# A four-layer diffusion trunk on one core: the gated MLP's preparation in four steps, two early weights for the last feed forward, and three more modulations of layer 2 on TensorE

## The chip, the cores and the metric

The kernel runs on one core of one Trainium2 chip. The metric is the device time of one launch in microseconds (us). Five engines run their own instruction streams and wait for one another: TensorE (PE, with its weight loads as PEld), VectorE (DVE), ScalarE (ACT), GpSimd (POOL) and SyncE (SP), which here issues the DMA transfers. Each engine takes its instructions strictly in program order, so what stands behind a waiting instruction waits too.

## The reference

A trunk of four layers over a sequence of 256 tokens and a context of 256 tokens, 1024 channels, all in float32. Each layer has a mixer (pooling, attention, a state-space model, a gated MLP in turn) and a feed forward with a convolution. Both are framed by modulations that a condition vector makes.

```python
for layer in range(DEPTH):                       # pool, attn, ssm, gmlp
    sh1, sc1, gt1, sh2, sc2, gt2 = split(silu(c) @ ada_w[layer] + ada_b[layer], 6)
    h = x * (1 + sc1) + sh1
    y = mixer[layer](h)
    x = layer_norm(ALPHA * x + gt1 * y)
    f = conv_ffn(x * (1 + sc2) + sh2)
    x = layer_norm(ALPHA * x + gt2 * f)
    # the context stream goes the same way while a later layer reads it

def conv_ffn(h):                                 # 1024 -> 2 * 2816 -> 1024
    a = conv3(h @ w_up) + conv_b
    return (a[:2816] * silu(a[2816:])) @ w_down

def gmlp_mixer(h):                               # chunks of 128 tokens, 8 heads
    u, v = split(gelu(h @ w_in + b_in), 2)
    v = layer_norm(v)
    gate = einsum('hpq,bnqhc->bnphc', w_s, v) + b_s
    return (u * gate) @ w_out
```

`silu(c) @ ada_w` is six products of a 1024-vector with a 1024x1024 matrix per layer; (l, m) below is product m of layer l.

## The kernel before, in words

Every large product is computed as three: a weight is split into a rounded high part wH (ACT, L170) and the rest wL (DVE, or POOL where the call says so, L171), the left side likewise into hH and hL (L527, L528), and `mm3` runs hH·wH, hL·wH and hH·wL (L229, L230, L231). `weight()` issues each weight's load on SP (L186) into one of four `raw` buffers and splits it into one of three slots; pieces are 128x1024 numbers, 512 KB. A list `self.early` can hold weights that were split before their turn. `ahead()` makes such weights out of other tiles: three `araw` buffers and one `gate` buffer, with the low part split on POOL.

The stages follow one another as layer 0's pooling and feed forward, attention, feed forward 1 (ffn(1), 750 to 1187 us), the state-space mixer (to 1326), feed forward 2 (to 1530), the gated MLP (to 1728) and feed forward 3 (to the end).

Two background queues run beside the feed forwards. `hook()` is called once per weight and takes steps from them by credits. The first queue holds the modulations (`ada_task`): each step loads 128 rows of `ada_w` into an `araw` buffer (L327; three buffers, which `ahead` also uses). Where `array(l, m)` is true, TensorE multiplies the rows by the condition two steps later (L320, `ada<-araw,cond`, four matmuls per step). Where it is false, VectorE multiplies and sums them (`adaS`: L337 for the first, L339 for the other seven), and one last step on TensorE adds over the partitions (L320, `adaS,ones`). The second queue (`ssm_tasks`) prepares the state-space mixer: chains of complex products on POOL (`ef`, `efp`, L1176 to L1183) that begin with a load of `prm`, and whose results TensorE reads (L1387, L1388, L1406). All of it has to be done when ffn(1) ends. The last products of ffn(1) lie in 1170 to 1187 us.

`gmlp_open` prepares what the gated MLP needs of `w_s`: the matrix wsn is transposed in two halves on TensorE (L1672), copied by ACT (L1674), split into wsH and wsL, and summed by a product with ones (L1678, copied by L1679). It is called whole before pair 2 of ffn(2).

`out_proj_steps` runs a mixer's last projection and the layer norm behind it (transposes L506, hH and hL), after which the next feed forward begins with `first_up`.

## Time and profile before

| what | value |
|---|---|
| median of 3 runs | 1935.31 us (1934.91 to 1938.88) |
| profiled execution's own time | 1940.46 us |
| its span, first to last instruction | 1938.7 us |
| mean granted TensorE clock | 0.96 |
| busy: PE | 1782.9 us (92%) |
| busy: PEld | 1466.6 us (76%) |
| busy: DVE | 1318.2 us (68%) |
| busy: ACT | 781.3 us (40%) |
| busy: POOL | 1080.3 us (56%) |

Busy time is an average over the stages. A stage is decided by the engine whose chain ends last there, which need not be the one that is busiest over the whole span. The granted clock is the share of full speed that the chip gave TensorE. A row of the timeline has start, duration, engine, line and tiles, and in brackets the idle time ahead of it with the instruction that ended that idle time.

### The profile page before, as it was taken

How to read it: one execution, taken by the hardware profiler on the slowest of the kernel's cores; microseconds unless marked ns; L12 is line 12 of the kernel's file. 1: busy time of each engine (PE TensorE's matmuls, PEld its weight loads, DVE VectorE, ACT ScalarE, POOL GpSimd, SP SyncE). 2: the span in 40 equal slices, each digit the busy share in tenths (PEclk: the TensorE clock that was granted, in tenths of full speed). 3: DMA queues.
4: the chain of work that ended last, by engine and by line, in shares of the span. 5: the costliest groups of instructions: out<-in, count | busy, mean ns of one | idle time of the engine just before them, and what ended most of it. 6: DMA issues, size and time to landing. Idle time of an engine off the chain costs nothing.

```text
span 1938.7 us, 31709 instructions
## 1 busy us (share of the span) xinstructions
PE 1782.9 (92%) x12188; PEld 1466.6 (76%) x12188; DVE 1318.2 (68%) x1853; ACT 781.3 (40%) x1289; POOL 1080.3 (56%) x1040
## 2 busy tenths in 40 slices
PE   6899999899999999999989998688899988979997
PEld 4687676677789878777767776458798878979997
DVE  4565545546677767654676747987879798778666
ACT  2253223224346644422422332234654454436553
POOL 2278104989862335751189998647654444246643
PEclk8899999999999999999989999889899989989999
DMA  9555565565321124566656556865878765547662
GB/s 365 185 156 183 174 190 181 197 206 184 121 87 38 45 80 100 180 189 187 210 194 220 177 186 207 250 222 182 267 273 276 254 222 186 171 154 262 205 188 85
DMA packets 241785, 360.28 MB, mean 186 GB/s; under 512 B 43353, under 2 KB 164825, under 8 KB 241634
## 3 DMA queue, kind: packets, MB, share of 16 engines
q1 hardware_dynamic: 241634, 358.26, 57.2%
q8 instruction: 96, 1.57, 0.3%
q14 instruction: 55, 0.45, 0.1%
HBM read 330.92 MB, written 27.29 MB: 185 GB/s over the span
## 4 chain that ended last, share of the span: by engine, by line
PE 56%; POOL 21%; DVE 11%; issue 4%; DMA 4%; ACT 2%; SPq 0%; POOLq 0%; DVEq 0%; ACTq 0%
PE ps L229 15%; PE ps L230 14%; PE ps L231 14%; POOL ef L1178 2%; DVE wL L171 2%; POOL efp L1182 2%; POOL ef L1181 2%; POOL ef L1183 2%; POOL cv L1824 2%; POOL ef L1176 2%; POOL efp L1177 2%; PE sc L991 1%; PE ps L939 1%; PE ada L320 1%; PE pv L1046 1%
## 5 line engine op out<-in xcount | busy, mean ns | idle before, releaser
L171 DVE TENSOR_TENSOR wL<-raw,wH 128x1024 fp32r<-128x1024 f32 x292 | 422.8, 1453 | 197.2 <-ACT wH L170 189.9
L229 PE MATMUL ps<-hH,wH 128*128 128x256 f32 (+1 forms) x1568 | 524.2, 335 | 9.9 <-ACT wH L170 5.5
L170 ACT ACTIVATE wH<-raw 128x1024 fp32r<-128x1024 f32 x341 | 358.2, 1056 | 419.2 <-PE ps L231 218.3
L231 PE MATMUL ps<-hH,wL 128*128 128x256 f32 (+1 forms) x1568 | 516.8, 330 | 4.5 <-DVE wL L171 4.5
L230 PE MATMUL ps<-hL,wH 128*128 128x256 f32 (+1 forms) x1568 | 518.0, 331 | 1.6 <-DVE hL L528 1.1
L229 PEld LDWEIGHTS ps<-hH,wH 128*128 128x128 f32 x1568 | 301.7, 193 | 52.1 <-issue 8.9
L231 PEld LDWEIGHTS ps<-hH,wL 128*128 128x128 f32 x1568 | 301.5, 193 | 31.3 <-DVE wL L171 4.8
L230 PEld LDWEIGHTS ps<-hL,wH 128*128 128x128 f32 x1568 | 302.6, 193 | 26.7 <-POOL xa L633 1.3
L1824 POOL TENSOR_TENSOR cv<-cv,cv 128x512 f32<-128x512 f32 (+1 forms) x88 | 110.2, 1257 | 224.8 <-ACT cv L1823 224.8
L229 PE MATMUL ps<-wH,gH 128*128 128x512 f32 (+1 forms) x552 | 220.6, 400 | 9.0 <-DVE cv L1796 7.2
L231 PE MATMUL ps<-wH,gL 128*128 128x512 f32 (+1 forms) x552 | 213.9, 392 | 2.4 <-POOL gL L1828 2.3
L230 PE MATMUL ps<-wL,gH 128*128 128x512 f32 (+1 forms) x552 | 215.8, 391 | 0.0
L171 POOL TENSOR_TENSOR wL<-raw,wH 128x1024 fp32r<-128x1024 f32 x49 | 127.2, 2596 | 110.1 <-ACT wH L170 90.0
L1793 ACT ACTIVATE cv<-ps,cw 128x512 f32<-128x512 f32 (+1 forms) x176 | 115.9, 666 | 164.1 <-PE ps L231 138.9
L1794 DVE SCALAR_TENSOR_TENSOR cv<-ps,cw,cv 128x510 f32<-128x510 f32 (+1 forms) x176 | 106.5, 609 | 106.1 <-ACT cv L1793 105.9
L339 DVE SCALAR_TENSOR_TENSOR adaS<-araw,cond,adaS 128x1024 f32<-128x1024 f32 x70 | 117.0, 1671 | 36.2 <-DMA araw<-in_ada_w_dram 36.0
L229 PEld LDWEIGHTS ps<-wH,gH 128*128 128x128 f32 x552 | 106.0, 192 | 41.1 <-issue 15.8
L231 PEld LDWEIGHTS ps<-wH,gL 128*128 128x128 f32 x552 | 105.8, 192 | 26.8 <-POOL gL L1828 3.3
L230 PEld LDWEIGHTS ps<-wL,gH 128*128 128x128 f32 x552 | 106.1, 192 | 21.0 <-issue 0.2
L1796 DVE SCALAR_TENSOR_TENSOR cv<-ps,cw,cv 128x510 f32<-128x510 f32 (+1 forms) x176 | 106.7, 612 | 4.3
L540 POOL TENSOR_SCALAR rs<-mv 128x1 f32<-128x1 f32 x26 | 8.2, 314 | 165.5 <-DVE mv L538 165.0
L1827 ACT ACTIVATE gH<-cv 128x512 fp32r<-128x512 f32 (+1 forms) x88 | 45.9, 521 | 117.6 <-POOL cv L1824 117.6
(434 smaller groups left out, 3322.9 us busy)
## 6 DMA issues: line engine op xcount, KB each, us to landing
araw<-in_ada_w_dram SPq DMA_DIRECT2D x184, 512.0 KB
raw<-in_ffn_w_up_dram SPq DMA_DIRECT2D x176, 512.0 KB
raw<-in_ffn_w_down_dram SPq DMA_DIRECT2D x88, 512.0 KB
raw<-in_gmlp_w_in_dram SPq DMA_DIRECT2D x32, 512.0 KB
fD<-ef SPq DMA_DIRECT2D x16, 512.0 KB
eD<-eo SPq DMA_DIRECT2D x16, 512.0 KB
raw<-in_gmlp_w_out_dram SPq DMA_DIRECT2D x16, 512.0 KB
raw<-in_attn_w_qkv_dram SPq DMA_DIRECT2D x12, 512.0 KB
```

Source lines behind the costliest of these rows:

```text
L170: self.nc.scalar.activation(h, x, AF.Copy)
L171: (eng or self.nc.vector).tensor_tensor(l, x, h.bitcast(F32), op=ALU.subtract)
L229: mm(ps, lhsT=w[0], rhs=x[0], start=first, stop=False)
L230: mm(ps, lhsT=w[0], rhs=x[1], start=False, stop=False)
L231: mm(ps, lhsT=w[1], rhs=x[0], start=False, stop=last)
L339: nc.vector.scalar_tensor_tensor(a, raws[k], self.cond[:, k, r:r + 1], a, op0=ALU.mult, op1=ALU.add)
L1176: eng.tensor_tensor(out[0], a[0], b[0], op=ALU.mult)
L1793: nc.scalar.activation(c, p3, AF.Identity, scale=cw[:, 1, h:h + 1], bias=cw[:, 3, h:h + 1])
L1794: nc.vector.scalar_tensor_tensor(c[:, :, 1:], p3[:, :, :255], cw[:, 0, h:h + 1], c[:, :, 1:], op0=ALU.mult, op1=ALU.add)
L1796: nc.vector.scalar_tensor_tensor(c[:, :, :255], p3[:, :, 1:], cw[:, 2, h:h + 1], c[:, :, :255], op0=ALU.mult, op1=ALU.add)
L1824: nc.gpsimd.tensor_tensor(cv[0, j], cv[0, j], cv[1, j], op=ALU.mult)
L1827: nc.scalar.activation(gH, c0, AF.Copy)
```

## The change

It has three parts, called (a), (b) and (c) below.

(a) `array` becomes true for (2, 2), (2, 3) and (2, 4). These three modulations, which VectorE summed in ffn(1), are made by TensorE.

(b) The gated MLP's preparation becomes a generator in four steps, taken before pairs 1, 2, 3 and 4 of ffn(2). The matrix wsn lies in a `gate` buffer and not in a `raw` buffer, and is loaded at the start; the copies lie in an `h32` tile.

(c) `out_proj_steps` also calls `ahead` for the gated MLP's last projection (where there are no extra slots), so the first two weights of ffn(3) are loaded and split into three `araw` buffers and one `gate` buffer while that projection runs.

```diff
     def array(self, l, m):
-        return l < 2 or l == 2 and m < 2
+        return l < 2 or l == 2 and m < 5
...
             if hf:
                 self.conv(l)
-            if hf and S == 2:
+            if hf and (S == 2 or not self.extra):
                 ahead = self.ahead([w for w, shape in self.first_up(l, 2)])
...
+        if S == 2 or not self.extra:
+            self.early = ahead
         if S == 2:
-            self.early = ahead
             self.post_T(made["n"][0])
...
         def steps():
+            wsn = self.t(self.main, [128, D], F32, "gate", 3).rearrange("p (h q) -> p h q", h=8)
+            nc.sync.dma_start(wsn, I["gmlp_w_s"][0].rearrange("h p q -> p h q"))
...
-            wsn = self.t(self.wp, [128, 8, 128], F32, "raw", 4)
-            nc.sync.dma_start(wsn, I["gmlp_w_s"][0].rearrange("h p q -> p h q"))
...
+            yield
             for i in range(2):
...
-                w32 = self.t(self.sm, [128, 512], F32, "tmp", 3)
+                w32 = self.t(self.sm, [128, 4, 128], F32, "h32", 2).rearrange("p a b -> p (a b)")
                 nc.scalar.activation(w32, ps, AF.Copy)
+                yield
...
-        self.between = steps
+        self.between = steps()
...
-                    if p == 2 and self.between:
-                        self.between()
-                        self.between = None
+                    if p and self.between:
+                        next(self.between, None)
```

In the changed file the lines behind L299 have numbers higher by one to four: L1672 is L1675 there, L1678 is L1682, L1794 is L1797, L1828 is L1831.

**Part (a): DVE and PE in ffn(1).** DVE in the program before, in the last products of ffn(1)'s up projection, where (2, 2) ends and (2, 3) begins:

```order
L1828 TENSOR_TENSOR gL_9126<-cv_1532_9011,gH_9125 128x512
L1796 SCALAR_TENSOR_TENSOR cv_1551_9119<-ps_9020,cw_7122,cv_1551_9119 128x2x255
L171 TENSOR_TENSOR wL_9293<-raw_9290,wH_9292 128x1024
L339 SCALAR_TENSOR_TENSOR adaS_9079<-araw_9483,cond_94,adaS_9079 128x1024
L1828 TENSOR_TENSOR gL_9132<-cv_1533_9015,gH_9131 128x512
L1794 SCALAR_TENSOR_TENSOR cv_1573_9232<-ps_9135,cw_7122,cv_1573_9232 128x2x255
L337 TENSOR_SCALAR adaS_9576<-araw_9577,cond_94 128x1024
L1796 SCALAR_TENSOR_TENSOR cv_1573_9232<-ps_9135,cw_7122,cv_1573_9232 128x2x255
```

The same place on DVE in the changed program:

```order
L1831 TENSOR_TENSOR gL_9125<-cv_1532_9011,gH_9124 128x512
L171 TENSOR_TENSOR wL_9297<-raw_9294,wH_9296 128x1024
L1831 TENSOR_TENSOR gL_9131<-cv_1533_9015,gH_9130 128x512
L1797 SCALAR_TENSOR_TENSOR cv_1573_9233<-ps_9134,cw_7122,cv_1573_9233 128x2x255
L1799 SCALAR_TENSOR_TENSOR cv_1573_9233<-ps_9134,cw_7122,cv_1573_9233 128x2x255
```

And a place on PE in the changed program, where a step of (2, 2) stands between the products of two weights (`ada`):

```order
L231 MATMUL ps_9135<-hH_105,wL_9181 128x512
L320 MATMUL ada_9081<-araw_9142,cond_94 32x256 x4
L229 MATMUL ps_9241<-hH_105,wH_9245 128x512
L230 MATMUL ps_9241<-hL_106,wH_9245 128x512
L231 MATMUL ps_9241<-hH_105,wL_9246 128x512
```

All 24 DVE instructions of the three modulations are gone, and 24 steps of this kind stand on PE (3 steps with `adaS` and ones are gone). The points at which PE takes POOL's `ef` stand between the same weights as before, but for one that stands seven products of `mm3` earlier.

**Part (b): PE in ffn(2).** Before, in the middle of pair 2's products:

```order
L231 MATMUL ps_13107<-hH_12309,wL_13145 128x256
L229 MATMUL ps_13108<-hH_12309,wH_13144 128x256
L1678 MATMUL bg_13092<-tmp_13088,ones_13076 128x512
L1672 MATMUL bg_13095<-ident_81,raw_13078 128x128 x4
L230 MATMUL ps_13108<-hL_11599,wH_13144 128x256
L231 MATMUL ps_13108<-hH_12309,wL_13145 128x256
```

After, between the state-space mixer's last products and the first of ffn(2):

```order
L243 MATMUL bg_12971<-ident_81,rowsT_12967 128x16 x3
L1675 MATMUL bg_13140<-ident_81,gate_12965 128x128 x4
L506 MATMUL ps_12744<-ident_81,xa_16_110 128x128 x4
L506 MATMUL ps_12745<-ident_81,xa_16_110 128x128 x4
L506 MATMUL ps_12774<-ident_81,xa_17_111 128x128 x4
L506 MATMUL ps_12775<-ident_81,xa_17_111 128x128 x4
L1682 MATMUL bg_13307<-h_2255_13145,ones_12977 128x512
L1675 MATMUL bg_13310<-ident_81,gate_12965 128x128 x4
L229 MATMUL ps_12819<-hH_12366,wH_12638 128x256
```

Both transposes of wsn and the first product with ones stand in the layer norm's gap; the second product with ones stands later, between two weights (at a place that ran at some 1419 us before). ACT's first copy stands ahead of the last two hH of the layer norm, its second copy and both wsH behind them. On SP the load of wsn stands before the state-space mixer's last products.

**Part (c): PE and DVE at the start of ffn(3).** PE before, the first products behind the layer norm's last transposes:

```order
L506 MATMUL ps_16915<-ident_81,xa_17_111 128x128 x4
L229 MATMUL ps_16954<-hH_12309,wH_16958 128x256
L230 MATMUL ps_16954<-hL_11599,wH_16958 128x256
L229 MATMUL ps_16955<-hH_12309,wH_16958 128x256
L230 MATMUL ps_16955<-hL_11599,wH_16958 128x256
L231 MATMUL ps_16954<-hH_12309,wL_16959 128x256
L231 MATMUL ps_16955<-hH_12309,wL_16959 128x256
```

PE after; the weight is read from `araw`:

```order
L506 MATMUL ps_16984<-ident_81,xa_17_111 128x128 x4
L229 MATMUL ps_17023<-hH_12366,araw_16675 128x256
L229 MATMUL ps_17024<-hH_12366,araw_16675 128x256
L230 MATMUL ps_17023<-hL_11656,araw_16675 128x256
L231 MATMUL ps_17023<-hH_12366,araw_16676 128x256
L230 MATMUL ps_17024<-hL_11656,araw_16675 128x256
L231 MATMUL ps_17024<-hH_12366,araw_16676 128x256
```

DVE before, behind the last two hL:

```order
L528 TENSOR_TENSOR hL_11599<-tmp_16930,hH_12309 128x4x128
L528 TENSOR_TENSOR hL_11599<-tmp_16935,hH_12309 128x4x128
L337 TENSOR_SCALAR adaS_16964<-araw_16965,cond_94 128x1024
L171 TENSOR_TENSOR wL_16959<-raw_16956,wH_16958 128x1024
L339 SCALAR_TENSOR_TENSOR adaS_16964<-araw_17042,cond_94,adaS_16964 128x1024
L171 TENSOR_TENSOR wL_16995<-raw_16992,wH_16994 128x1024
```

DVE after:

```order
L528 TENSOR_TENSOR hL_11656<-tmp_17004,hH_12366 128x4x128
L171 TENSOR_TENSOR wL_17094<-raw_17091,wH_17093 128x1024
L171 TENSOR_TENSOR wL_17129<-raw_17126,wH_17128 128x1024
L171 TENSOR_TENSOR wL_17183<-raw_17180,wH_17182 128x1024
L171 TENSOR_TENSOR wL_17256<-raw_17253,wH_17255 128x1024
L1797 SCALAR_TENSOR_TENSOR cv_2960_17081<-ps_17023,cw_16671,cv_2960_17081 128x255
L1797 SCALAR_TENSOR_TENSOR cv_2961_17085<-ps_17024,cw_16671,cv_2961_17085 128x255
L1799 SCALAR_TENSOR_TENSOR cv_2960_17081<-ps_17023,cw_16671,cv_2960_17081 128x255
L1799 SCALAR_TENSOR_TENSOR cv_2961_17085<-ps_17024,cw_16671,cv_2961_17085 128x255
L337 TENSOR_SCALAR adaS_17027<-araw_17028,cond_94 128x1024
L339 SCALAR_TENSOR_TENSOR adaS_17027<-araw_17099,cond_94,adaS_17027 128x1024
```

The first two weights' low parts are made on POOL, in the out projection, behind the gated MLP's last `gt` product (L1759 there) and ahead of the layer norm's L540. Four more weights of ffn(3) are split one behind the other on DVE right behind hL, and the modulation's L337 and L339 stand behind the first convolutions. On SP the first two weights' loads stand among the loads of the last projection's weights; the loads for modulation (3, 5) stood between the first weights of ffn(3) (1704.78 and 1710.43 us) and stand behind six of its weights now.

## Rows read from the trace of the kernel before

**Rows 1.** The page's fourth part: the chain that ended last, share of the span by engine.

```profile
PE 56%; POOL 21%; DVE 11%; issue 4%; DMA 4%; ACT 2%; SPq 0%; POOLq 0%; DVEq 0%; ACTq 0%
```

**Rows 2.** Windows: us, busy us of PE, PEld, DVE, ACT, POOL, granted clock, DMA share.

```profile
977.00:1170.00 193.00, 175.39 (x1181) 136.50 (x1180) 128.61 (x116) 61.74 (x96) 182.86 (x128) 0.95 0.56 191
...
1365.00:1385.00 20.00, 12.53 (x74) 10.71 (x74) 17.84 (x21) 13.42 (x23) 15.98 (x9) 0.74 0.83 267
...
1720.00:1745.00 25.00, 14.29 (x88) 12.97 (x88) 22.38 (x23) 12.13 (x20) 18.89 (x13) 0.73 0.33 111
```

**Rows 3.** Groups of PE, 950 to 1200: busy, mean ns, idle before, releaser.

```profile
L1406 PE MATMUL bg<-ident,ef 128*128 128x128 f32 x64 | 9.1, 275 | 2.6 <-POOL ef L1183 2.6
...
L1387 PE MATMUL bg<-ef,prm 64*32 64x112 f32 x128 | 6.8, 284 | 14.5 <-POOL ef L1183 11.4 <-POOL ef L1178 3.1
```

**Rows 4.** Timeline of POOL, 1058 to 1067: start, us, instruction.

```profile
1062.39 2.04 POOL L1181 TENSOR_TENSOR ef<-prm 128x512 f32<-128x512 f32 x1
...
1064.74 1.06 POOL L1177 TENSOR_TENSOR efp<-prm 128x512 f32<-128x512 f32 x1
```

**Rows 5.** Timeline of DVE in the same stretch.

```profile
1061.78 1.73 DVE L339 SCALAR_TENSOR_TENSOR adaS<-araw,cond,adaS 128x1024 f32<-128x1024 f32 x1 [0.27 <-DMA araw<-in_ada_w_dram]
```

**Rows 6.** Groups of DVE, 977 to 1171.

```profile
L339 DVE SCALAR_TENSOR_TENSOR adaS<-araw,cond,adaS 128x1024 f32<-128x1024 f32 x13 | 22.7, 1747 | 14.4 <-DMA araw<-in_ada_w_dram 14.4
```

**Rows 7.** The chain of waits, 862 to 872: start, us, what.

```profile
868.33 0.24 PE ps L231
868.57 0.57 PE ada L320 x8
869.14 0.43 PE ps L229
```

**Rows 8.** Instructions of line L320 in 750 to 1187, and what their engine waited for.

```profile
L320 PE MATMUL ada<-araw,cond x192: 379/379/404, 789.0 to 943.7; 128*32 128x256 f32 x192
...
  DMA raw<-in_ffn_w_up_dram: 0.4, 1
```

**Rows 9.** The chain of waits, 955 to 1000.

```profile
971.55 5.74 DMA prm<-prmD
977.50 1.06 POOL ef L1176
```

**Rows 10.** Timeline of PE, 1364 to 1386.

```profile
1364.95 0.27 PE L229 MATMUL ps<-hH,wH 128*128 128x256 f32 x1
1372.69 2.08 PE L1678 MATMUL bg<-tmp,ones 128*128 128x512 f32 x2 [7.47 <-ACT tmp L1674]
...
1378.13 0.28 PE L231 MATMUL ps<-hH,wL 128*128 128x256 f32 x1
```

**Rows 11.** Groups of ACT, 1330 to 1400.

```profile
L170 ACT ACTIVATE wH<-raw 128x1024 fp32r<-128x1024 f32 x19 | 19.8, 1052 | 14.1 <-DMA raw<-in_ffn_w_up_dram 10.7 <-PE ps L230 3.4
...
L1674 ACT ACTIVATE tmp<-bg 128x512 f32<-128x512 f32 x2 | 1.2, 588 | 0.0
```

**Rows 12.** Timeline of SP's DMA issues, 1340 to 1352.

```profile
1344.90 0.37 SPq L1664 DMA_DIRECT2D raw<-in_gmlp_w_s_dram  x1
1350.49 0.37 SPq L186 DMA_DIRECT2D raw<-in_ffn_w_up_dram  x1
```

**Rows 13.** Timeline of PE, 1325 to 1345.

```profile
1333.08 0.77 PE L229 MATMUL ps<-hH,wH 128*128 128x256 f32 x4 [2.43 <-ACT hH L527]
```

**Rows 14.** Timeline of PE, 1715 to 1745.

```profile
1728.77 0.58 PE L229 MATMUL ps<-hH,wH 128*128 128x256 f32 x1 [3.90 <-ACT wH L170]
...
1734.64 0.80 PE L231 MATMUL ps<-hH,wL 128*128 128x256 f32 x2 [4.50 <-DVE wL L171]
```

**Rows 15.** Timeline of DVE, 1715 to 1745.

```profile
1727.28 3.42 DVE L528 TENSOR_TENSOR hL<-tmp,hH 128x512 fp32r<-128x512 f32 x2 [1.01 <-ACT hH L527]
...
1736.72 7.88 DVE L171 TENSOR_TENSOR wL<-raw,wH 128x1024 fp32r<-128x1024 f32 x4
```

**Rows 16.** Timeline of POOL, 1670 to 1735.

```profile
1717.62 0.19 POOL L540 TENSOR_SCALAR rs<-mv 128x1 f32<-128x1 f32 x1 [40.65 <-DVE mv L538]
```

## The prediction

> **What bounds the kernel now.** I read the page's chain first. PE has 56% of it and POOL 21% [rows 1]: PE decides most stages, so work on POOL or DVE counts only in the stages where PE waits. The windows by stage say where that is. In 977 to 1170 (most of ffn(1)) PE is busy for 175.4 of 193 us and POOL for 182.9, at a granted clock of 0.95; in 1365 to 1385 PE works for 12.5 of 20 us at 0.74, in 1720 to 1745 for 14.3 of 25 us at 0.73 [rows 2]. These are the three places that the change touches, one for each part. The groups of PE name what it waits for in ffn(1): L1406 and L1387 stood idle for 2.6 and 14.5 us, all of it for POOL's `ef` [rows 3]. So the 17.6 us of idle time there are POOL's chain, which begins when `prm` lands at 977.5 [rows 9]. In ffn(2) a single wait of 7.47 us stands ahead of L1678 [rows 10], and at ffn(3)'s start there are two, 3.90 us for wH and 4.50 us for wL of the first weight [rows 14].
>
> **Part (a), PE's side.** A step of four matmuls has 0.57 us in the chain, and the product behind it 0.43 us, where the product ahead has 0.24 [rows 7]: 0.57 + 0.19 = 0.76 us. Twenty-four steps are 18.2 us; the three dropped steps with ones have the same form and give back 2.3. Net PE work: +15.9 us. The room for it is PE's idle time in 977 to 1170, 17.6 us, and what the clock lost, at most 0.05 x 193 = 9.7 us [rows 2]. If POOL made it wait for nothing more, the stretch would become 17.6 + 9.7 - 15.9 = 11.4 us shorter.
>
> **Part (a), POOL's side.** POOL's products of one shape take 1.06 us alone (L1177) and 2.04 us (L1181) [rows 4] where DVE's L339 runs beside them [rows 5]. So one L339 costs POOL about 1.0 us, and 13 of them stand in the stretch [rows 6]. That is 13 us at most; some of the 13 meet the gap between two products or share it with a split that would slow it anyway, so I take 10. Against it, the order puts the issues that lead to `prm` behind one more weight's load on SP. The nearest row for such a turn is the 5.74 us of `prm`'s own landing [rows 9]; a transfer that only queues adds less, and I take 3. POOL's chain would then end 7 us sooner; bounds 13 sooner (no delay) to 5.7 later (no relief).
>
> The Trainium skill ("SBUF — State Buffer", Who interferes with whom) says that a DVE instruction with two SBUF inputs and a GpSimd instruction that reads SBUF exclude each other for the whole instruction. By that rule POOL would gain up to the 22.7 us that the 13 L339 lasted [rows 6], and PE alone would set the end, at -11.4. The row's own 1.0 us for an L339 of 1.73 us is less, and the sum goes by the row.
>
> Both ends, PE's -11.4 and POOL's -7, are for one of them alone. PE takes POOL's results at some 18 points between fixed weights, and at each the later one counts; with both so near, part of each gain is lost at such points. I take **-5 us**, range -11.4 to +5.7.
>
> The DVE instructions that go leave nothing on the path by themselves: L339 waited 14.4 us for its loads [rows 6], so DVE had time. The same loads now feed PE; that is rival 1.
>
> **Part (b).** PE's last product before the stall ends at 1365.2, and the clock is back at full speed with the product at 1378.13 [rows 10]. In these 12.9 us it did the two products with ones, four transposes and some 13 products that belong to the stage. The latter have 256 columns; at half of the 0.24 us of a 512-column product [rows 7] they are worth 1.6 us. So 11.3 us go if nothing takes their place. What comes back: ACT's copy (0.59 us, [rows 11]) now stands ahead of the hH for which PE waits 2.43 us in the layer norm's gap [rows 13], and PE's transposes and the product with ones (2.08 us for two at the low clock, [rows 10]) stand in that gap, mostly in time that PE waits. I count 0.6 + 1.2 = 1.8 us. That leaves -9.5. Then the weights: ACT waited 10.7 us for raw loads in 1330 to 1400 [rows 11], with the DMA engines at 0.83 in the stall itself [rows 2], and PE now comes to the next weights 9.5 us sooner. On the other side wsn no longer holds a raw buffer; its load at 1344.90 was the only one of that ring until the next weight's at 1350.49 [rows 12]. Two splits of ws also move on DVE into the stretch at 1342 to 1348, ahead of weights. I let these give back 3 us: **-6.5 us**. Bounds: -9.5 (nothing given back) and -2 (the loads had hardly any more to give, and three quarters return as waits for weights).
>
> **Part (c).** With both halves of the first weights ready, the 4.50 us for wL go, and of the 3.90 us the last 1.0, in which ACT makes wH after its last hH [rows 14, 15]. What is late next is hL: DVE makes the last two from 1727.28 to 1730.70 [rows 15], and the products of the second half of the tokens need the first of them at some 1729.0. PE starts with the others, so I take 0.5 us for that. The splits that follow do not become the bound: before, DVE made four of them in 7.88 us from 1736.72 on [rows 15], after, four from 1730.7 on, since L337 and L339 stand behind them. The two splits on POOL cost nothing there, since POOL is idle for 40.65 us until 1717.62 [rows 16]. The loads cost the last projection's ring two turns; nothing in the rows prices it, and between 0 and 4.5 us (the whole gain) I take 0, since the clock and the DMA share of 0.33 behind it [rows 2] show no queue. Sum: -4.5 - 1.0 + 0.5 = **-5 us**, range -6 to -1.
>
> **The sum** is -5 - 6.5 - 5 = -16.5 us. On the profiled execution's own 1940.46 us that is 1924.0. That execution lay 5.15 us above the median of 1935.31 (outside the three runs, of which the slowest was 1938.88), so against the median the forecast is 1935.3 - 16.5 = **1918.8 us**.
>
> **Rival 1, slower: TensorE waits for the modulations' loads.** PE takes its steps in order, so a load that is late holds every product behind it. DVE waited 14.4 us for the same loads in this stretch [rows 6]. If PE waits as long, it needs 175.4 + 15.9 + 14.4 = 205.7 us, 12.7 more than now, and each wait costs clock: behind the 7.47 us of [rows 10] 5.4 us ran at half speed, 2.7 lost; for some ten shorter waits I put 4 in all. Then (a) is +17, and with (b) and (c) the kernel ends at 1935.3 + 17 - 11.5 = 1940.8. It decides against the change once these waits, with the clock, pass 15 us. Against it: the 24 steps of this kind before [rows 8] waited 0.4 us for a DMA, and that for a weight; they use loads two steps ahead.
>
> **Rival 2: POOL's chain gains nothing.** The later start and other two-input work on DVE eat the relief. POOL's chain ends as before, PE hides its 15.9 us in the waits, and (a) is 0: 1935.3 - 11.5 = 1923.8. For it: 4 of the 13 us suffice to be lost beyond those I took off.
>
> **Rival 3: the weights are the bound behind both removed stalls.** (b) falls to -2 and (c) to -1, because loads or DVE's splits come no sooner. With (a) at -5: 1935.3 - 8 = 1927.3. For it speaks the 10.7 us of [rows 11].
>
> **Rival 4: everything at its good end.** -11.4 - 9.5 - 5.5 = -26.4: 1908.9.
>
> **How the numbers follow.** A change under 0.2% (3.9 us) cannot be told from none here. Chances: the forecast 0.48 (its own range 1912 to 1925), rival 2 0.20, rival 3 0.16, rival 4 0.07, rival 1 0.09. Of rival 1, about a third falls within 0.2%; of rival 3, where (a) fails too (-3), about a fifth. So faster 0.87, same 0.06, slower 0.07. The range runs from 1909 to 1930: it holds the forecast and rivals 2 and 3, and leaves out rival 1, half of rival 4 and the tail of rival 3.
>
> **What would show it.** (a): L320 with `araw,cond` as 192 more records in ffn(1) with hardly any idle time ahead of them; no L339 before 1170; POOL's products there mostly at 1.05 us; ffn(1) some 5 us shorter, and the waits on `ef` below 12 us. (b): no wait of several us near 1365, the granted clock there at 1.0, the gap of the layer norm at 1333 longer by 1 to 2 us, and waits for wH or wL near 1360 to 1375 of less than 4 us together. (c): no L231 that waits for wL at ffn(3)'s start, `araw` as the first products' weight, and PE through the first two weights some 5 us sooner, measured from the last L506. The forecast is wrong if PE waits ahead of L320, if `prm` lands more than 6 us later, or if the two removed stalls turn up again as waits for weights within the next 20 us.

## The result, and the profile after

The changed kernel took 1927.33 us (median of 4 runs, 1926.3 to 1929.7), the kernel before 1937.1 us beside it (4 runs, 1934.91 to 1939.25): a ratio of 0.9949, 95% interval 0.9932 to 0.9966, 7 to 13 us less. A second series gave 1923.64 us against 1935.48 us, 0.9938 (0.9920 to 0.9956). The forecast was 16.5 us less, with 1918.8 us as the time and 1909 to 1930 us as its range; 9.8 us less were measured, and the time lies near the slow end of the range.

To see where the time went I took from PE's timeline the start of each layer norm's first transposes (L555, L506) and the differences between them, in the profiles of before, of the change and of the twelve runs below, one profile each. "POOL order" is explained at the second experiment.

| kernel | ffn(1) | ffn(2) | gated MLP | ffn(3) to the end | POOL order |
|---|---|---|---|---|---|
| before | 446.4 | 226.8 | 166.3 | 218.8 | rs rs v v |
| changed | 441.0 | 227.3 | 165.6 | 215.5 | rs rs v v |
| e1: (a) | 439.4 | 225.7 | 167.9 | 222.7 | rs v rs v |
| e2: (b) | 446.1 | 229.0 | 169.5 | 219.8 | rs v rs v |
| e3: (c) | 444.6 | 230.7 | 165.9 | 214.7 | rs rs v v |
| e4: (a), (c) | 441.4 | 226.6 | 171.3 | 220.6 | rs v rs v |
| e5: changed again | 441.0 | 223.9 | 165.7 | 215.3 | rs rs v v |
| e6: splits later | 439.2 | 222.4 | 165.7 | 215.3 | rs rs v v |
| e7: sums kept | 458.4 | 228.9 | 169.1 | 219.3 | rs v rs v |
| e8: products left out | 429.1 | 226.8 | 165.5 | 221.6 | rs rs v v |
| e9: two inputs | 455.7 | 226.5 | 168.5 | 222.4 | rs v rs v |
| e10: one input | 437.7 | 226.2 | 168.7 | 220.0 | rs v rs v |
| e11: (a), (b) | 439.3 | 225.5 | 166.5 | 222.5 | rs rs v v |
| e12: (b), (c) | 447.8 | 228.6 | 170.9 | 214.6 | rs v rs v |

ffn(1) is 5.4 us shorter in the changed kernel's profile, ffn(3) 3.3 us, and ffn(2) is 0.5 us longer. The first 74.4 us of the profile of before were 69 to 72 us in all others; that is a part of why its own time lay above the median.

The three stretches of the forecast, in the windows of the changed kernel (columns as in [rows 2]):

```profile
974.00:1162.00 188.00, 180.60 (x1328) 135.82 (x1326) 98.96 (x101) 61.21 (x95) 168.82 (x129) 0.98 0.64 207
1340.00:1366.00 26.00, 20.59 (x155) 19.90 (x155) 22.16 (x22) 12.08 (x18) 22.58 (x12) 0.93 0.75 252
1712.00:1737.00 25.00, 19.93 (x135) 18.46 (x134) 20.10 (x24) 13.75 (x23) 21.14 (x15) 0.80 0.39 123
```

The first answers to 977 to 1170 in [rows 2]: 188 us in place of 193, PE busy for 180.6, POOL for 168.8 in place of 182.9, DVE for 99.0 in place of 128.6, the clock at 0.98. PE is the bound there now. The groups of PE in 942 to 1192 of the changed kernel:

```profile
L320 PE MATMUL ada<-araw,cond 128*32 128x256 f32 x192 | 14.7, 390 | 0.0
...
L1388 PE MATMUL bg<-ef,prm 64*32 64x112 f32 x128 | 6.0, 273 | 7.4 <-POOL ef L1184 6.9 <-POOL ef L1179 0.5
```

The 192 records of L320 are the 24 added steps, with no idle time ahead of them. PE's wait for `ef` went from 17.1 us [rows 3] to 7.4. POOL's timeline in the changed kernel shows the relief, and who waits now:

```profile
1051.21 1.98 POOL L1177 TENSOR_TENSOR ef<-prm 128x512 f32<-128x512 f32 x1 [2.45 <-PE bg L1389]
1053.15 1.06 POOL L1182 TENSOR_TENSOR ef<-prm 128x512 f32<-128x512 f32 x1
```

L1182 (L1181 before) takes 1.06 us where L339 stood beside it before [rows 4]; and the product ahead of it had to wait 2.45 us for PE.

In ffn(2) the 7.47 us of [rows 10] are gone. PE's timeline in the changed kernel has these waits instead, in the layer norm's gap and behind it:

```profile
1325.74 2.07 PE L1682 MATMUL bg<-h,ones 128*128 128x512 f32 x2 [2.15 <-ACT h L1677]
```

```profile
1347.53 0.36 PE L229 MATMUL ps<-hH,wH 128*128 128x256 f32 x1 [1.04 <-DVE cv L1799]
...
1350.30 0.36 PE L229 MATMUL ps<-hH,wH 128*128 128x256 f32 x1 [2.18 <-DVE cv L1799]
```

```profile
1449.62 0.69 PE L367 MATMUL bg<-ident,adaP 128*128 128x128 f32 x2 [3.29 <-ACT adaP L353]
```

The first stands where PE waited 2.43 us for hH before [rows 13], and it cost nothing: counted from the layer norm's first transposes, the 24th product of the stage ends at 12.8 us, 12.7 before. The next two, with a third of 1.88 us at 1365.00, end with DVE's convolutions (L1799). What DVE did until then, from its timeline:

```profile
1337.66 1.79 DVE L171 TENSOR_TENSOR wsL<-h,wsH 128x512 fp32r<-128x512 f32 x1
1339.37 3.41 DVE L339 SCALAR_TENSOR_TENSOR adaS<-araw,cond,adaS 128x1024 f32<-128x1024 f32 x1
1342.70 1.77 DVE L171 TENSOR_TENSOR wsL<-h,wsH 128x512 fp32r<-128x512 f32 x1
1344.40 2.07 DVE L171 TENSOR_TENSOR wL<-raw,wH 128x1024 fp32r<-128x1024 f32 x1
1346.39 0.47 DVE L1797 SCALAR_TENSOR_TENSOR cv<-ps,cw,cv 128x255 f32<-128x255 f32 x1
...
1347.69 2.07 DVE L339 SCALAR_TENSOR_TENSOR adaS<-araw,cond,adaS 128x1024 f32<-128x1024 f32 x1
1349.69 0.47 DVE L1799 SCALAR_TENSOR_TENSOR cv<-ps,cw,cv 128x255 f32<-128x255 f32 x1
```

DVE worked without a gap: splits, the two new wsL and L339, each 1.8 to 3.4 us long, stand ahead of the convolutions for which PE waits. Ahead of the third wait DVE itself was held up, by the load for a modulation's L339 that stands in front of the convolution:

```profile
1360.16 2.63 DVE L339 SCALAR_TENSOR_TENSOR adaS<-araw,cond,adaS 128x1024 f32<-128x1024 f32 x1 [2.12 <-DMA araw<-in_ada_w_dram]
```

PE's products, counted from the layer norm in both profiles, show what became of the gain. At the 168th product the changed kernel is 4.8 us later than before, at the 240th, behind the place of the stall, 6.8 us sooner. So the stall's removal gave 11.6 us, close to the 11.3 of the forecast. From the 264th product to the 408th the lead is 5.3 us, at the 792nd 3.6; behind the late copy at 1449 it is 1.5 us at most, and the stage ends 0.5 us later than before.

At ffn(3)'s start (PE, then DVE, in the changed kernel), the two waits of [rows 14] became 1.97 and 1.09 us, the second for hL:

```profile
1719.68 0.79 PE L229 MATMUL ps<-hH,araw 128*128 128x256 f32 x2 [1.97 <-ACT hH L527]
1721.56 0.55 PE L230 MATMUL ps<-hL,araw 128*128 128x256 f32 x1 [1.09 <-DVE hL L528]
```

```profile
1719.66 3.45 DVE L528 TENSOR_TENSOR hL<-tmp,hH 128x512 fp32r<-128x512 f32 x2 [0.55 <-ACT hH L527]
1723.03 6.76 DVE L171 TENSOR_TENSOR wL<-raw,wH 128x1024 fp32r<-128x1024 f32 x3
```

The three splits behind hL begin at 1723.03, 3.37 us after hL did; before, one begins 5.03 us after it (at 1732.31) and the four in [rows 15] 9.44 us. Counted from the layer norm's first transposes, the 48th product of ffn(3) ends at 16.9 us, 22.5 before.

### The profile page after: what moved, and what is told of

It reads as the page before. It is cut to its first block, busy times and chain, and to the rows that moved or that the text cites. A ratio compares the mean times of both kernels' runs of the same rounds, so it can differ in the third digit from the quotient of the medians.

```text
span 1927.9 us, 32057 instructions
## 1 busy us (share of the span) xinstructions
PE 1790.0 (93%) x12356; PEld 1465.1 (76%) x12356; DVE 1278.3 (66%) x1827; ACT 782.1 (41%) x1289; POOL 1079.1 (56%) x1042
## 4 chain that ended last, share of the span: by engine, by line
PE 57%; POOL 15%; DVE 13%; issue 5%; DMA 4%; ACT 3%; SPq 0%; POOLq 0%; DVEq 0%; ACTq 0%
PE ps L229 15%; PE ps L231 14%; PE ps L230 14%; DVE wL L171 3%; POOL cv L1827 2%; PE ada L320 2%; DVE adaS L339 2%; PE sc L992 1%; PE ps L940 1%; PE pv L1047 1%; POOL efp L1183 1%; POOL ef L1179 1%; POOL ef L1182 1%; POOL ef L1184 1%; DMA araw<-in_ada_w_dram 1%
## 5 line engine op out<-in xcount | busy, mean ns | idle before, releaser
L229 PE MATMUL ps<-hH,wH 128*128 128x256 f32 (+1 forms) x1552 | 518.1, 335 | 9.6 <-DVE cv L1799 8.4
L230 PE MATMUL ps<-hL,wH 128*128 128x256 f32 (+1 forms) x1552 | 510.2, 329 | 0.5 <-DVE hL L591 0.5
L231 PE MATMUL ps<-hH,wL 128*128 128x256 f32 (+1 forms) x1552 | 509.4, 329 | 0.8 <-POOL wL L171 0.8
L229 PEld LDWEIGHTS ps<-hH,wH 128*128 128x128 f32 x1552 | 296.5, 192 | 54.4 <-issue 14.6
L231 PEld LDWEIGHTS ps<-hH,wL 128*128 128x128 f32 x1552 | 296.8, 191 | 27.2 <-POOL wL L171 1.0
L230 PEld LDWEIGHTS ps<-hL,wH 128*128 128x128 f32 x1552 | 297.1, 191 | 24.9 <-issue 1.0
L1827 POOL TENSOR_TENSOR cv<-cv,cv 128x512 f32<-128x512 f32 (+1 forms) x88 | 115.0, 1312 | 211.4 <-ACT cv L1826 211.3
L1797 DVE SCALAR_TENSOR_TENSOR cv<-ps,cw,cv 128x510 f32<-128x510 f32 (+1 forms) x176 | 106.5, 609 | 126.5 <-ACT cv L1796 126.2
L1799 DVE SCALAR_TENSOR_TENSOR cv<-ps,cw,cv 128x510 f32<-128x510 f32 (+1 forms) x176 | 106.6, 612 | 4.3
L339 DVE SCALAR_TENSOR_TENSOR adaS<-araw,cond,adaS 128x1024 f32<-128x1024 f32 x49 | 84.1, 1716 | 13.1 <-DMA araw<-in_ada_w_dram 12.9
L1017 POOL TENSOR_SCALAR araw<-araw,den 128x512 f32<-128x512 f32 (+1 forms) x64 | 40.8, 654 | 86.5 <-ACT gate L1034 19.2
```

The source lines that it names most:

```text
L229: mm(ps, lhsT=w[0], rhs=x[0], start=first, stop=False)
L230: mm(ps, lhsT=w[0], rhs=x[1], start=False, stop=False)
L231: mm(ps, lhsT=w[1], rhs=x[0], start=False, stop=last)
L339: nc.vector.scalar_tensor_tensor(a, raws[k], self.cond[:, k, r:r + 1], a, op0=ALU.mult, op1=ALU.add)
L1017: nc.gpsimd.tensor_scalar(pt[:, e, i], pt[:, e, i], den[:, e, i:i + 1], 1.0, op0=ALU.mult, op1=ALU.mult)
L1797: nc.vector.scalar_tensor_tensor(c[:, :, 1:], p3[:, :, :255], cw[:, 0, h:h + 1], c[:, :, 1:], op0=ALU.mult, op1=ALU.add)
```

## The experiments

### Each part alone, and the change without its second part (e1 to e4)

e1 has only this line of the change, e2 the preparation in steps (the hunks of `gmlp_open` and `ffn`), e3 only the hunks of `out_proj_steps`, e4 those of e1 and e3.

```diff
-        return l < 2 or l == 2 and m < 2
+        return l < 2 or l == 2 and m < 5
```

> Only part (a), the three modulations of layer 2 on TensorE. Theory 1 (each part is worth what its place shows in the trace of the changed kernel): ffn(1) was 5.0 us shorter there, so this kernel is 5 us faster than before, and its POOL products beside the old L339 places run at 1.05 us, with the stretch from prm's landing to ffn(1)'s last products some 188 us long. Rival (the predicted term was right only by luck, the parts interact): (a) alone gives 0 to 2 us because nothing behind ffn(1) takes the time up.

> Only part (b), the preparation in four steps. Theory 1: ffn(2) as a whole was not shorter in the changed kernel (226.8 us before, 227.3 after, between the two layer norms' first transposes), since three waits for convolutions (5.1 us) and one for a modulation's copy (3.3 us) took the place of the stall; so (b) alone gives 0 to -1 us. Rival (the loss at the modulation's copy is a chance meeting that only the combined program has): (b) alone shows the waits for convolutions but not the later one, and gives -5 to -6 us.

> Only part (c), the first two weights of the last feed forward split early. Theory 1: the last feed forward began 3.3 us sooner relative to its layer norm in the changed kernel, of which a peak of 5.6 us was there behind the second weight; so (c) alone gives -3 to -3.5 us. Rival (POOL's splits or the two turns of the ring cost the last projection something that the changed kernel hid): (c) alone gives 0 to -1 us, with waits in the last projection.

> Parts (a) and (c) without (b): the changed kernel with the preparation as before. Theory 1: -5 - 3.3 = -8.3 us against before, so within 1 to 2 us of the changed kernel, with the 7.5 us stall back in ffn(2) and neither the waits for convolutions near 1347 and 1365 nor the one near 1449. Rival ((b) is worth its -5 to -6 us): this kernel is 5 us slower than the changed one.

Measured against 1935.32 us of before: e1 1934.71 us (0.9991, 0.9980 to 1.0002), e2 1942.08 (1.0025, 1.0011 to 1.0039), e3 1929.65 (0.9975, 0.9962 to 0.9987), e4 1936.42 (0.9998, 0.9984 to 1.0012). Only e3 is near what was expected, and gains more than that. The stages hold what theory 1 said of (a): 439.4 and 441.4 us in ffn(1). But the gain does not arrive at the end, and for e2 and e4 both theory 1 and its rival missed: (b) alone costs 5 us by its ratio (7 by the medians), and (a) with (c) gains nothing, though all three together gain ten. In e2 the waits came as its rival said, 4.32 and 2.94 us for convolutions in ffn(2) and none at the later copy, but the time did not. So theory 1 falls as a sum over places.

### Where the parts alone lose: an order in the gated MLP

The table shows it: the gated MLP, which no part's diff touches behind its preparation, takes 168 us or more in e1, e2 and e4. POOL's timeline of e1 in that stage:

```profile
1601.34 1.04 POOL L540 TENSOR_SCALAR rs<-mv 128x1 f32<-128x1 f32 x1 [26.59 <-DVE mv L538]
...
1603.22 5.37 POOL L1726 TENSOR_SCALAR v<-v,mv,rs 128x1024 f32<-128x1024 f32 x1
1608.67 0.19 POOL L540 TENSOR_SCALAR rs<-mv 128x1 f32<-128x1 f32 x1
...
1609.63 4.32 POOL L1726 TENSOR_SCALAR v<-v,mv,rs 128x1024 f32<-128x1024 f32 x1
```

And that of e3:

```profile
1606.27 1.43 POOL L540 TENSOR_SCALAR rs<-mv 128x1 f32<-128x1 f32 x2 [31.25 <-DVE mv L538]
...
1608.85 8.99 POOL L1727 TENSOR_SCALAR v<-v,mv,rs 128x1024 f32<-128x1024 f32 x2
```

In e3, as before and after the change, both small `rs` stand ahead of both large `v` (L1726 and L1727, 5 and 4 us each). In e1 the second `rs` stands behind the first `v`. Who waits for it, on DVE and then on PE, in e1:

```profile
1609.55 0.81 DVE L1726 TENSOR_SCALAR v<-v,mv,rs 128x1024 f32<-128x1024 f32 x1 [2.49 <-POOL rs L541]
...
1617.44 0.60 DVE L1753 SCALAR_TENSOR_TENSOR gt<-ps,gvec,tmp 128x128 f32<-128x128 f32 x2
```

```profile
1618.09 0.38 PE L229 MATMUL ps<-hH,wH 128*128 128x256 f32 x1 [2.10 <-DVE gt L1753]
```

DVE's `v` waits 2.49 us for the late `rs`, the chain behind it ends in `gt` 7.9 us later, and PE waits 2.10 us for that; e3 has no such wait. The code of this stage is the same in both; the order of its instructions on an engine is made when the program is built. That it goes by an estimate of when each engine is free, which a change in ffn(1) or ffn(2) shifts, is how I explain the difference and is not shown. All seven profiles with `rs rs v v` have 165.5 to 166.5 us in this stage, all seven with `rs v rs v` 167.9 to 171.3. PE waits for that `gt` in all of the latter, by 1.15 to 2.54 us, and in none of the former. In e4, the longest, the wait is 2.10 us as in e1, and the granted clock in the 40 us behind it is 0.92, where it is 1.00 in the changed kernel. The fourteen profiles hold only five different orders of DVE in this stage, two of the short kind and three of the long.

In ffn(3), DVE's order is one and the same in the changed kernel and e3, and another in e4, where the stage took 220.6 us. But e4 had what (c) is for: its two waits at the start are as short as e3's (2.43 and 1.09 us), and its 48th product ends at 16.4 us, as in e3. It lost that again to DVE's convolutions, for which e3 waits 1.19 us at most (PE in e4):

```profile
1769.75 0.55 PE L229 MATMUL ps<-hH,wH 128*128 128x256 f32 x1 [3.61 <-DVE cv L1797]
...
1780.92 0.36 PE L229 MATMUL ps<-hH,wH 128*128 128x256 f32 x1 [2.97 <-DVE cv L1797]
```

e1 has two such waits there too, of 1.28 and 2.11 us, and 222.7 us in ffn(3); that costs it more than the gated MLP does. An order of its own does not have to cost: e12's in ffn(3) differs from e3's as well, and its stage took 214.6 us.

### The same with two pairs of parts (e11, e12)

e11 is (a) with (b), e12 (b) with (c). Their instruction orders were known ahead of the run.

> Parts (a) and (b) without (c). Theory 3 (the order in which the program places the untouched instructions of the gated MLP on DVE sets that stage's length, whatever parts are in): this program has there the same order as the changed one, so the stage takes 165.7 us within 0.7 us; ffn(1) is 5 us shorter than before, the last feed forward 218 to 222 us without (c); in all 1929 to 1933 us. Rival (the stage's length is chance, or a cost of (a) that (c) takes back): the stage takes 168 us or more, as with (a) alone and (a) with (c).

> Parts (b) and (c) without (a). Theory 3: this program has the gated MLP's DVE order of (b) alone, where the stage took 169.5 us, so it takes 169.5 us within 1 us again, some 3.5 us more than before; ffn(1) is as before, and what (c) gains at the end is about lost there: 1932 to 1937 us. Rival (as above): 165.5 to 166.5 us, and 1928 us.

Measured against 1937.16 us: e11 1931.20 us (0.9959, 0.9944 to 0.9974), e12 1934.56 (0.9999, 0.9983 to 1.0015). The gated MLP took 166.5 and 170.9 us: both on the side that theory 3 gave them, 0.1 and 0.4 us outside its margins. e11's ffn(3), 222.5 us, lies just above its 218 to 222; both totals are as expected. So theory 3 is borne out by a forecast in both directions, and its rival is not; no run changed this order and nothing else.

### The changed kernel again, and wsL later (e5, e6)

e6 holds steps 3 and 4 behind the last convolution of the pair before:

```diff
-                        next(self.between, None)
+                        with self.behind(self.last_cv if p > 2 else None):
+                            next(self.between, None)
```

> The changed kernel once more, with more runs, beside the three below. Theory 2 (the parts do not add up, since behind ffn(1) DVE and POOL meet in other phases in each program and each execution): its median lies within 3 us of the 1927.3 us measured first, its runs spread over 6 us or more as those of the single parts did, and its profile again has ffn(1) 4 to 6 us shorter than before, while the stages behind it differ by several us from the first profile. Rival (the first result was a lucky draw, as (a) with (c) gave nothing): 1932 to 1936 us.

> The changed kernel with steps 3 and 4 of the preparation held behind the last convolution of the pair before, which in the instruction order moves DVE's two wsL splits behind the first convolutions of ffn(2) and leaves PE as it is. Theory 2: the waits for convolutions near 1347 to 1365 (5.1 us and the clock behind them) come from those splits, 1.8 us each, so most of them goes and the kernel is 3 to 5 us faster than the changed one. Rival (the weights' loads bound that place anyway, ACT waited 7.5 us for one at 1350): the waits change their name, to wH or wL, and the time stays within 1.5 us.

Measured against 1935.48 us: e5 1923.64 us (its runs 1920.4 to 1925.9), e6 1922.99 (0.9932, 0.9912 to 0.9952). e5 refutes the rival: the gain is real (its median 0.7 us outside the expected 3, its spread 5.4 where 6 or more was expected). The two profiles of the one program differ by 3.4 us in ffn(2). Where this begins can be read on DVE and POOL, which make one split each at the same time, ahead of the same convolutions. In the changed kernel's first profile:

```profile
1435.67 3.44 DVE L171 TENSOR_TENSOR wL<-raw,wH 128x1024 fp32r<-128x1024 f32 x1
```

```profile
1435.63 2.40 POOL L171 TENSOR_TENSOR wL<-raw,wH 128x1024 fp32r<-128x1024 f32 x1 [0.83 <-ACT wH L170]
```

In e5:

```profile
1432.93 1.21 DVE L171 TENSOR_TENSOR wL<-raw,wH 128x1024 fp32r<-128x1024 f32 x1
```

```profile
1432.91 3.50 POOL L171 TENSOR_TENSOR wL<-raw,wH 128x1024 fp32r<-128x1024 f32 x1 [0.85 <-ACT wH L170]
```

Both start within 0.04 us of each other. In the first POOL's split takes 2.40 us and DVE's 3.44; in e5 DVE's takes 1.21 us and POOL's 3.50. One keeps its length, and the other is longer by about as much. Where DVE lost, its convolutions came 2.2 us later, and a modulation's copy behind them on ACT 2.9 us later (from the split's start): that is the wait of 3.29 us at 1449.62, which e5 does not have. e5 kept 2.9 us of (b)'s gain to the end of ffn(2), against before. In e6 theory 2 fell: the wsL splits are gone from the place, its median is 0.7 us from e5's, yet PE waits for convolutions there by 1.04, 1.21 and 3.09 us, as much as before. DVE's timeline in e6:

```profile
1331.39 2.32 DVE L339 SCALAR_TENSOR_TENSOR adaS<-araw,cond,adaS 128x1024 f32<-128x1024 f32 x1
1333.64 3.41 DVE L171 TENSOR_TENSOR wL<-raw,wH 128x1024 fp32r<-128x1024 f32 x1
1336.97 0.47 DVE L1798 SCALAR_TENSOR_TENSOR cv<-ps,cw,cv 128x255 f32<-128x255 f32 x1
```

Ordinary splits and L339 fill the time as well, one of them 3.41 us long. Ahead of the 3.09 us, DVE again stood idle for a modulation's load, 1.99 us. So it is not the wsL alone, but all that stands on DVE there, with that load. The rival's loads, those of the weights, are not it: the time stayed as the rival said, but the waits did not become waits for wH or wL.

### What pays for (a): four kernels that differ in ffn(1) (e7 to e10)

All four are (a) alone, with an addition or omission that concerns ffn(1). In e7 VectorE still makes the sums, which nothing reads:

```diff
+            if idle and k < KT:                  # l == 2 and 1 < m < 5
+                with self.tc.issue_after(self.last_hT.ins):
+                    if k == 0:
+                        nc.vector.tensor_scalar(dum, raws[k], ...)
+                    else:
+                        nc.vector.scalar_tensor_tensor(dum, raws[k], ..., dum, ...)
```

e8 leaves out seven of the eight steps of each of the three modulations:

```diff
-                if k >= lag:
+                if k >= lag and not (skip and k < KT + lag - 1):
```

e9 and e10 add two DVE instructions behind the first half of each complex product on POOL (e9 the first form, e10 the second):

```diff
+ nc.vector.scalar_tensor_tensor(dum[:, q * 512:q * 512 + 512], o[:, 0], self.cond[:, q, 0:1], o[:, 0], ...)
+ nc.vector.bn_stats(dst[:, q, :], o[:, 0])
```

> Part (a) alone, with TensorE's steps, but VectorE still makes the same 24 sums, which nothing reads. Theory 2 (POOL's relief is what pays for TensorE's 16 us): POOL's products are slowed again, its busy time in the stretch goes back to some 183 us, TensorE waits for ef by 10 us or more again, and ffn(1) is 5 us or more longer than with (a) alone, so no shorter than before. Rival (TensorE's own waits go for another reason, the place or the start of POOL's chain): ffn(1) stays within 1.5 us of (a) alone.

> Part (a) alone, with 21 of its 24 TensorE steps left out (the three modulations are then made of their last rows only): neither engine does that work. Theory 2 (after the change TensorE is the bound of ffn(1), with 7.4 us of waits left): the 21 steps at 0.76 us are 16 us less work, waits for POOL come back, and ffn(1) is 4 to 8 us shorter than with (a) alone. Rival (POOL still bounds ffn(1)): within 1.5 us of (a) alone.

> Part (a) alone, and DVE makes 42 extra scalar_tensor_tensor instructions of 128x512 with two SBUF inputs, in pairs, each pair behind the first half of one of POOL's complex products in ffn(1); nothing reads them, and they wait for no load. Theory 2 (POOL's products lose time to such DVE instructions beside them, about as much as these last): with 21 pairs of 1.28 us, POOL's busy time in the stretch is 15 to 25 us higher than with (a) alone (164.6 us), and ffn(1) is 8 to 15 us longer than its 439.4 us. Rival (the 18 us that the kept sums cost came from the araw buffers that they held, not from POOL): ffn(1) within 3 us.

> The same with 42 bn_stats instructions of 128x512 in the same places, which read one SBUF input: as many DVE instructions, in the same order, of about the same length. Theory 2: POOL's busy time stays within 4 us of that with (a) alone, and ffn(1) within 3 us of 439.4 us. Rival (DVE's being busy, and what is late behind it, costs the time): as with the two-input instructions.

e7 took 1950.88 us against 1935.48 (1.0077, 1.0057 to 1.0097): ffn(1) is 19 us longer than in e1. PE's groups in 961 to 1210:

```profile
L322 PE MATMUL ada<-araw,cond 128*32 128x256 f32 x176 | 13.9, 401 | 4.4 <-DMA araw<-in_ada_w_dram 4.4
L1414 PE MATMUL bg<-ident,ef 128*128 128x128 f32 x64 | 9.2, 279 | 5.0 <-POOL ef L1191 5.0
L1395 PE MATMUL bg<-ef,prm 64*32 64x112 f32 x128 | 6.2, 282 | 3.9 <-POOL ef L1191 3.9
```

POOL's busy time in the whole of ffn(1) is back to 291.4 us, as before the change (291.3; e1 has 277.2), so it was DVE's sums that lengthened POOL's products. 8.9 us of waits for POOL's `ef` stand there, where e1 has 7.1, but also 4.4 us for the loads, whose buffers DVE now holds, and 4.3 for a copy on ACT. So e7 alone does not say which of these made the 19 us. e9 and e10 leave the loads out; each ran once, in 1952.34 and 1930.07 us. The rows are DVE's extra work and the window of 192 us that ends 22 us ahead of ffn(1)'s layer norm. In e9:

```profile
L1371 DVE SCALAR_TENSOR_TENSOR adaS<-ef,cond 128x512 f32<-128x512 f32 x38 | 59.4, 1598 | 37.7 <-POOL ef L1178 37.7
```

```profile
979.57:1171.57 192.00, 174.75 (x1277) 129.72 (x1276) 148.79 (x128) 59.07 (x92) 172.49 (x124) 0.96 0.58 194
```

and in e10:

```profile
L1371 DVE BATCH_NORM_STATS2 dumst<-ef 128x6 f32<-128x512 f32 x37 | 23.9, 684 | 55.2 <-POOL ef L1178 55.2
```

```profile
960.92:1152.92 192.00, 186.11 (x1354) 139.10 (x1353) 115.30 (x133) 64.32 (x98) 166.13 (x127) 0.97 0.64 210
```

With the same places and counts, e9's ffn(1) is 455.7 us, 16.3 longer than e1's, e10's 437.7, 1.7 shorter. The two-input instruction took 1598 ns on the mean, the one-input one 684. That is POOL's doing: the few in e9 that met no POOL product, or only began before one, took 739 to 752 ns, the others 1527 to 1785. Two neighbours in e9, of which the first ran beside POOL and the second alone:

```profile
1069.19 1.66 DVE L1371 SCALAR_TENSOR_TENSOR adaS<-ef,cond 128x512 f32<-128x512 f32 x1 [1.62 <-POOL ef L1178]
...
1072.47 0.74 DVE L1371 SCALAR_TENSOR_TENSOR adaS<-ef,cond 128x512 f32<-128x512 f32 x1
```

POOL's busy time rose by 7.9 us and by 1.5 (e1's is in the row below); for e9 that is half of what was expected. The rest went another way: DVE's 59.4 us held up its convolutions, for which PE waited 9.6 us in ffn(1), where it waited 2.4 in e1, and POOL too. So 42 more DVE instructions cost nothing here when they read one input. How much of e9's 16.3 us came through POOL and how much through DVE, whose extra work lasted 35.5 us longer than e10's, is not separated; both come from the meeting of the two engines. e1 and e8 in the same window, in this order:

```profile
961.46:1153.46 192.00, 184.82 (x1353) 138.13 (x1352) 97.59 (x97) 64.54 (x99) 164.62 (x126) 0.98 0.64 208
```

```profile
952.86:1144.86 192.00, 182.62 (x1245) 143.12 (x1244) 106.65 (x103) 67.11 (x103) 165.98 (x126) 0.99 0.61 204
```

e8 took 1921.18 us (0.9927, 0.9909 to 0.9944), and its ffn(1) is 10.3 us shorter than e1's, more than the 4 to 8 expected; PE's waits for POOL, which were to come back, did not (7.3 us, e1 7.1). So PE's steps are what bounds ffn(1) after (a). The 21 steps left out took 13.2 us off PE's busy time in the stage (428.1 to 414.9), at most 0.63 us a step, with the clock at 0.992 in e1 and 0.996 in e8.

## Why the prediction was right, and where it was off

**The side, and what bounds.** The three places were the right ones. In ffn(1), leaving out e7 to e10, the six profiles with (a) have 440.2 us on the mean (439.2 to 441.4), the four without it 446.2 us (444.6 to 447.8).

**(a), forecast -5, measured -6.0** by these means. Its two sides: PE's step was priced by the rows at 0.76 us, and of the 15.9 us of added work only 6.2 show in PE's busy time of the whole stage (429.7 us in 738 to 1179 of the changed kernel, 423.5 in 741 to 1187 before). The clock rose there from 0.973 to 0.988, some 7 us of 441; the rest is the step's price, 0.63 us by e8, so 13 us net and not 15.9. POOL's relief was mis-sized low: its busy time in the window of 192 us fell from 178.5 to 164.0 us, 14.5, where I took 10 and gave 13 as the most, and the later start that I set against it (3 us) did not come: `ef` began 236.1 us behind attention's layer norm, 236.5 before. That moved the bound to PE, which the forecast had as one of its two ends; that TensorE might wait for the modulations' loads (rival 1) did not happen.

The Trainium skill ("SBUF — State Buffer", Who interferes with whom) says that a DVE instruction with two SBUF inputs contends with a GpSimd instruction that reads SBUF, and that one with at most one SBUF input, outside the two-port modes, does not. e9 and e10 agree with it: 1598 against 684 ns an instruction, 455.7 against 437.7 us in ffn(1).

**(b), forecast -6.5, measured about nothing.** ffn(2) took 226.9 us on the mean of the five profiles with (b) as it is (changed, e2, e5, e11, e12: 223.9 to 229.0), and 227.3 on that of five without it (before, e1, e3, e4, e8: 225.7 to 230.7). By these means it lies outside the -9.5 to -2 that I gave. The step that failed is "I let these give back 3 us": the stall's removal was as read (11.6 us where 11.3 were forecast), but in the changed kernel 6.3 of them were given back by the 408th product and all by the end of the stage. I looked for the bound behind it at the loads and at ACT; it was DVE. Before, DVE was busy for 17.8 of the 20 us around the stall [rows 2], with splits, L339 and convolutions; now such splits, and L339 with its loads, stand ahead of the convolutions for which PE waits. The waits are for convolutions, which the text did not name; e6 shows that the wsL are not to blame alone. How much is left depends on the execution, nothing in the first profile and 2.9 us in e5, and on the order: e2 and e12, without (a), share POOL's order in ffn(2) and have the same waits for convolutions, 4.3 and 2.9 us.

**(c), forecast -5, measured -3.3** in the first pair of profiles and -6.0 by the means: 215.1 us with it (changed, e3, e5, e6, e12: 214.6 to 215.5) against 221.1 without (before, e1, e2, e8, e11: 218.8 to 222.7), with e4 as the exception at 220.6. At the place itself there is no exception: the 48th product ends 16.4 to 17.0 us behind the layer norm in all six with (c), 21.7 to 22.7 in the five without, 5.3 us sooner on the mean. The limit behind it was hL, as said. What the stage keeps of that depends on the waits for convolutions that follow: of the changed kernel's 5.6 us some 2.4 went again.

**The sum.** -6, nothing and -6 make -12, against the -7 to -13 of the first interval. The range held the time because the gain of (b) was the only term that failed, and by luck in the gated MLP's order: with e4's 171.3 us there in place of 165.6, the time would by estimate have been 1933 us, outside it. Rival 3 gave 1927.3 us, which is the time, but with (b) at -2 and (c) at -1 and late weights as the reason: the number was met by other terms than its own. What I did not consider at all is that the same edit can change the order of stages that it does not touch, which goes with 2 to 5 us in the gated MLP (e1, e2, e4, e12) and, through the convolutions in ffn(3), with 4 to 5 us more in e1 and e4. One slip in the text: rival 2 says that 4 us of POOL's relief lost would make (a) worth 0. By its own sum it takes 7, since 10 less 3 were left.

Open: why e2 as a whole is 5 to 7 us slower. Its profile has 3.2 us more in the gated MLP, 2.2 in ffn(2) (with a wait of 4.32 us for a convolution at 1353.17) and 1.1 in ffn(3); I did not try to bring its order to that of before, so the shares are read and not shown by a run.

## What to carry to other kernels

When a stall is removed, price the next bound on every engine that worked through the stall, not only on the one that was waiting: here VectorE had caught up in it. Where the build places instructions, compare the order of the stages that the edit leaves alone, before and after: with one small instruction behind a 5 us one, a stage took 2 to 5 us longer, against gains of some 6 us a part, and the parts did not add up. Work with two SBUF inputs on VectorE was paid twice here while GpSimd was the bound; moving it to TensorE at some 0.63 us a step was worth it until TensorE became the bound itself.

## What the runs showed of the hardware that was not expected

A program's executions differ by more than the effects sought: e11's 12 runs span 1924.2 to 1938.7 us. When a split on VectorE and one on GpSimd started within 0.04 us of each other, one execution of a program gave 1.21 us to VectorE and 3.50 to GpSimd, another 3.44 and 2.40. PE was 4.3 us later for it at 1449 and 3.4 us later at the end of the stage. And the hold between VectorE and GpSimd is costly on both sides: the 38 extra two-input instructions in e9's window took 59.4 us on DVE where 37 one-input ones of as many columns took 23.9 us, and two of e9's that ran alone took 0.74 us each.
